# The expert stage on one Trainium2 core: per-expert lists of 64 slots, two experts side by side in the array, weights multiplied as plain 32-bit numbers

## The chip, the cores and the metric

The kernel runs on 1 core of one Trainium2 chip. The metric is device time in microseconds (us) from the first to the last instruction of one execution. TensorE (PE) does the matrix products, VectorE (DVE), ScalarE (ACT) and GpSimd (POOL) the elementwise work; SyncE (SP) only issues transfers. PEld is the loading of PE's stationary operand, which runs beside PE.

## The reference, cut to what matters

One block with a mixture of experts is followed by two layers of another block (dense feed-forward networks "ffn" and mixers). The change is inside the experts: 256 tokens of 1024 features, 16 experts in 4 groups, each expert with three 32-bit weight matrices (gate and up 1024 x 512, down 512 x 1024, 6 MB in all, 96 MB for the 16).

```
pg = softmax(t @ w_group + b_group); gsel = argmax(pg)           # one group per token
pe = softmax((t @ w_expert + b_expert)[the 4 experts of gsel])
top_p, top_i = top_k(pe, 2)                                       # two experts of that group
gates = one_hot(...) * pg_sel * top_p / sum(top_p)
for e in range(16):
    h = silu(t @ w_gate[e]) * (t @ w_up[e])
    y = y + gates[:, e:e + 1] * (h @ w_down[e])
```

A token uses 2 of 16 experts, so an expert has 32 tokens on average. In the drawn inputs the largest group has 80 tokens and the largest expert 43.

## The kernel before

The token rows lie in two tiles X[0], X[1] of 128 tokens by 1024 features. Phases run in a fixed order: `block1` (the first mixer, ending with `out_proj`), `moe` (the experts, `_moe`), then `ffn` and `mix` of the two later layers. Instructions are written in program order with two kinds of raised priority (`AHEAD` for loads, `urgent` for short work that frees a bank), and a scheduler makes one fixed order for each engine out of it; at run time each engine goes through its order and waits on semaphores.

Weights come in chunks of 1 MB (128 partitions x 2048 numbers) through SP's queue. Eight places hold raw chunks during the experts: 5 called `more`, 3 called `raw`. In `load`, ACT copies a chunk, 1024 columns at a time, into a rounded "high" part (`hi`, type fp32r), DVE subtracts to get the "low" part (`lo`), and a raw place is free when its parts are made. There are 5 places for `hi` and 5 for `lo`. A product of 32-bit accuracy is then three PE products, high by high, high by low, low by high (`mm3`).

For the experts, `moe_enter` turns X into high and low parts token by token and computes the router's products while `out_proj` finishes; `route` finds the group of each token and its place in the group's list of 128 slots; `moe_pass` builds a selection matrix `pm`, gathers the features of the slots by products with it (`gather`), and goes through the experts one by one: `half` (gate, then up), `hidden` (silu and gate weight), `hidden_T` (transposes) and `down`. All 128 slots of a group pass through each of its four experts, and the slot's gate weight is 0 where the token did not choose the expert. The outputs of the four experts add up in two banks `acc`; once per group `place` scatters them back into X. Then the first weights of the next ffn are fetched (`load_apart`, `prefetch`), and a second pass stands behind a branch that is taken only if a group has over 128 tokens (not the case here).

Of the kernel before, what the change touches and what calls it, by code (L numbers as in the profile page):

```python
# [10 lines left out]
F32 = mybir.dt.float32  # L11
# [8 lines left out]
P = 128  # L20
# [11 lines left out]
NMORE = 5  # L32


# ---------------------------------------------------------------- host layout
# [170 lines left out]
class Kern:  # L206
# [50 lines left out]
    # weights: one transfer, then exact high and low parts  # L257
# [21 lines left out]
    def load_apart(self, ap):  # L279
        """the same with its parts among the places of more_raw"""  # L280
# [18 lines left out]
    def rsqrt(self, out, ss, scale, n, pool=True):  # L299
        """out = (ss * scale + EPS) ** -0.5 for small [128, n]"""  # L300
# [10 lines left out]
    def newton(self, out, v, y, c):  # L311
        """out = v ** -0.5; y, c: places"""
# [31 lines left out]
    def half_parts(self, h):  # L344
        """places for high and low parts of four tiles of 128 features"""
# [6 lines left out]
    def enter(self, h):  # L352
        """for the phase to come: half h of X^T with its gain per feature, split"""
# [21 lines left out]
    def inv_rms(self, pool=True):  # L375
        """1 / rms of the rows of X: [128, TB]"""
# [11 lines left out]
    def bcast(self, inv, pool=None):  # L388
        """per-token scalars [128, TB] as rows over all partitions [128, T]"""
# [13 lines left out]
    def final_norm(self, fp):  # L403
        """X * its 1 / rms * gain; returns the product of 1 / rms before and after"""
# [11 lines left out]
    def _ffn(self, fp, ap, final):  # L416
# [4 lines left out]
        # the first gate and up tiles start on the first half of X^T  # L421
# [63 lines left out]
    # ------------------------------------------------------------ block 1  # L485
# [6 lines left out]
    def projA(self, w_ap, xh, xl, tag="wk", between=None):  # L492
        """512 output columns, token-major: two banks"""
# [12 lines left out]
    def _block1(self, mp):  # L506
# [3 lines left out]
        # values, token-major  # L510
# [24 lines left out]
        # lower bound of the forget gate  # L535
# [13 lines left out]
        # hgrn2: f, q feature-major  # L549
# [31 lines left out]
        # fox projections and the gate, between the levels of hgrn2  # L581
# [48 lines left out]
        # hgrn2 output  # L630
# [84 lines left out]
    def fox_cum(self, mp, xh, xl, invb):  # L715
        """cumulative log forget per head, as rows"""
# [26 lines left out]
    def values65(self, mp):  # L743
        """values of 8 heads with a column of ones each, 96 columns readable from every head on"""
# [92 lines left out]

    def moe_enter(self, n, t):
        """half n of X[t] is final: its parts, token-major, and a step later its transposes and router products"""
# [33 lines left out]
        with self.urgent():  # L873
            nc.scalar.copy(hi[:, t], x)
            (nc.gpsimd if last else nc.vector).tensor_tensor(lo[:, t], x, hi[:, t].bitcast(F32), op=OP.subtract)

    def _moe(self, mp):
        nc = self.nc
        with self.urgent():
            inv = self.inv_rms(False)  # L880
# [7 lines left out]
        with self.tc.If(n > P):  # L888
            self.moe_pass(mp, R, 1)
        self.ready, self.nmore = ready, NMORE  # L890

    def first_max(self, mp, name, p, also=None):
        """largest of 4 and the one-hot of its first place: p [128, TB, 4]"""
        nc = self.nc
        m = mp.tile([P, TB, 1], F32, name=name + "m")
        nc.vector.tensor_reduce(m[:, :, 0], p, axis=AX.X, op=OP.max)
        sc = mp.tile([P, TB, 4], F32, name=name + "s")
        nc.vector.tensor_tensor(sc, p, m.to_broadcast([P, TB, 4]), op=OP.is_equal)
        nc.vector.tensor_tensor(sc, sc, self.cfs("w4").unsqueeze(1).to_broadcast([P, TB, 4]), op=OP.mult)
        ms = mp.tile([P, TB, 1], F32, name=name + "k")  # L900
        nc.vector.tensor_reduce(ms[:, :, 0], sc, axis=AX.X, op=OP.max)
        oh = mp.tile([P, TB, 4], F32, name=name + "o")
        if also is not None:
            nc.vector.tensor_tensor(also, sc, ms.to_broadcast([P, TB, 4]), op=OP.is_equal)
        nc.vector.tensor_tensor(oh, sc, ms.to_broadcast([P, TB, 4]), op=OP.is_equal)
        return m, oh

    def route(self, mp, inv):
        nc = self.nc
# [4 lines left out]
        L = mp.tile([P, TB, 20], F32, name="L")  # L914
# [964 lines left out]
```

## Time and profile before

| | |
|---|---|
| median of 3 runs | 1732.8 us (1731.53 to 1735.16) |
| the profiled execution, its span | 1732.4 us |
| PE busy | 97% of the span |
| ACT, DVE, POOL busy | 54%, 73%, 10% |
| bytes moved by transfers | 320.43 MB, 185 GB/s on average |
| experts: first gather product to last addition to X | 182.6 to 485.5 us |

The span is the whole of the profiled execution; it lies 0.4 us under the median of the runs. Busy shares are averages over all phases, and PE's rows overlap each other, since the next product starts before the one before it has left the array; the distance between starts is therefore the better measure of a product's cost.

### The profile page before, as it was taken

The page shows a single profiled execution, that of the slowest core. Times are in us where ns is not written, and L with a number is a line of the kernel's source. Part 1 is how long each engine was busy: PE and PEld are TensorE (multiplying, and loading weights), DVE is VectorE, ACT ScalarE, POOL GpSimd, SP SyncE. Part 2 cuts the span into 40 slices and gives each one's busy share as a digit, 9 for nine tenths or more (in the row PEclk, how much of TensorE's full clock was granted, in tenths as well). Part 3 has the DMA queues.
Part 4 walks back from the last instruction along what each step waited for, and adds up shares of the span by engine and source line. Part 5 has one row for each costly group of instructions (what it writes and reads, how often), then busy time and mean ns, then how long its engine had stood idle before and what let it go on. Part 6 is the DMA issues. An engine that isn't in the chain of part 4 may idle for free.

```text
span 1732.4 us, 26642 instructions
## 1 busy us (share of the span) xinstructions
PE 1673.2 (97%) x10679; PEld 1484.0 (86%) x10679; DVE 1261.2 (73%) x1829; ACT 939.9 (54%) x1409; POOL 176.7 (10%) x149
## 2 busy tenths in 40 slices
PE   8998799999989999999899999999999999899999
PEld 7986688887789998999679999899998997689998
DVE  5966889998866567888776565665658987876655
ACT  5545577776754445755445444544448554454443
POOL 0321100000000000122440000000001215320000
PEclk9999899999999999999899999999999999999999
DMA  9332599998685532543225555555554432245552
GB/s 383 112 101 87 201 348 360 364 351 310 244 315 177 176 137 90 181 138 113 91 73 178 188 188 177 171 180 183 194 171 151 168 122 98 73 148 184 191 183 99
DMA packets 46212, 320.43 MB, mean 185 GB/s; under 512 B 5376, under 2 KB 5632, under 8 KB 8704
## 3 DMA queue, kind: packets, MB, share of 16 engines
q1 hardware_dynamic: 45504, 318.04, 51.6%
q8 instruction: 86, 1.41, 0.3%
q10 hardware_dynamic: 576, 0.60, 0.1%
q14 instruction: 46, 0.38, 0.1%
HBM read 317.58 MB, written 1.05 MB: 184 GB/s over the span
## 4 chain that ended last, share of the span: by engine, by line
PE 61%; DVE 7%; ACT 2%; issue 1%; POOL 0%; ACTq 0%; DVEq 0%
PE wk L295 10%; PE wk L296 10%; PE wk L297 10%; PE acc L295 9%; PE acc L297 9%; PE acc L296 9%; DVE lo L274 1%; ACT hi L273 1%; PE wk L1759 1%; DVE xs L1336 1%; PE wk L1740 1%; DVE ol L1402 1%; PE wk L1524 0%; DVE m L1533 0%; PE wk L340 0%
## 5 line engine op out<-in xcount | busy, mean ns | idle before, releaser
L274 DVE TENSOR_TENSOR lo<-raw,hi 128x1024 fp32r<-128x1024 f32 (+1 forms) x380 | 458.7, 1223 | 208.2 <-ACT hi L273 202.5
L273 ACT CAST hi<-raw 128x1024 fp32r<-128x1024 f32 (+2 forms) x414 | 426.2, 1044 | 337.9 <-PE wk L296 121.7
L295 PE MATMUL wk<-xh,hi 128*128 128x256 f32 x1344 | 380.9, 283 | 0.0
L297 PE MATMUL wk<-xh,lo 128*128 128x256 f32 x1344 | 380.3, 283 | 0.0
L296 PE MATMUL wk<-xl,hi 128*128 128x256 f32 x1344 | 380.3, 283 | 0.0
L296 PEld LDWEIGHTS wk<-xl,hi 128*128 128x128 f32 x1344 | 256.7, 191 | 1.8
L295 PEld LDWEIGHTS wk<-xh,hi 128*128 128x128 f32 x1344 | 256.7, 191 | 1.7
L297 PEld LDWEIGHTS wk<-xh,lo 128*128 128x128 f32 x1344 | 256.7, 191 | 0.0
L274 DVE TENSOR_TENSOR lo<-more,hi 128x1024 fp32r<-128x1024 f32 x184 | 222.3, 1239 | 46.9 <-ACT hi L273 44.7
L273 ACT CAST hi<-more 128x1024 fp32r<-128x1024 f32 x186 | 190.1, 1049 | 81.3 <-PE acc L297 26.1
L295 PE MATMUL acc<-xh,hi 128*128 128x256 f32 x688 | 199.6, 292 | 0.1
L297 PE MATMUL acc<-xh,lo 128*128 128x256 f32 x688 | 194.8, 283 | 1.7 <-DVE lo L274 1.7
L296 PE MATMUL acc<-xl,hi 128*128 128x256 f32 x688 | 194.8, 284 | 0.5 <-DVE xl L370 0.4
L295 PE MATMUL acc<-hi,hh 128*128 128x512 f32 x352 | 139.5, 398 | 0.4 <-ACT hh L445 0.3
L296 PE MATMUL acc<-lo,hh 128*128 128x512 f32 x352 | 138.6, 395 | 0.0
L297 PE MATMUL acc<-hi,hl 128*128 128x512 f32 x352 | 137.4, 395 | 0.0
L295 PEld LDWEIGHTS acc<-xh,hi 128*128 128x128 f32 x688 | 131.1, 191 | 3.1 <-issue 1.3
L297 PEld LDWEIGHTS acc<-xh,lo 128*128 128x128 f32 x688 | 131.5, 191 | 2.4 <-DVE lo L274 2.2
L296 PEld LDWEIGHTS acc<-xl,hi 128*128 128x128 f32 x688 | 131.6, 191 | 1.9 <-DVE xl L370 0.9
L296 PE MATMUL wk<-lo,xgh 128*128 128x512 f32 x248 | 98.2, 396 | 2.0 <-DVE lo L274 1.8
L295 PE MATMUL wk<-hi,xgh 128*128 128x512 f32 x248 | 99.0, 399 | 0.0
L297 PE MATMUL wk<-hi,xgl 128*128 128x512 f32 x248 | 98.1, 396 | 0.0
(462 smaller groups left out, 2747.3 us busy)
## 6 DMA issues: line engine op xcount, KB each, us to landing
raw<-in_ffn_dram SPq DMA_DIRECT2D x111, 1024.0 KB, 4.8
more<-in_wmoe_dram SPq DMA_DIRECT2D x60, 1024.0 KB, 6.0
raw<-in_win_dram SPq DMA_DIRECT2D x37, 1024.0 KB, 4.8
raw<-in_wmoe_dram SPq DMA_DIRECT2D x36, 1024.0 KB, 6.2
more<-in_ffn_dram SPq DMA_DIRECT2D x21, 1024.0 KB, 4.9
raw<-in_wout_dram SPq DMA_DIRECT2D x17, 1024.0 KB, 4.8
more<-in_win_dram SPq DMA_DIRECT2D x7, 1024.0 KB, 11.0
raw<-in_wlat_dram SPq DMA_DIRECT2D x4, 896.0 KB, 4.6
```

What stands on the lines that cost most here:

```text
L273: nc.scalar.copy(hi[:, :sub], raw[:, s])
L274: (eng or nc.vector).tensor_tensor(lo[:, :sub], raw[:, s], hi[:, :sub].bitcast(F32), op=OP.subtract)
L295: nc.tensor.matmul(out, ah, bh, start=start, stop=False)
L296: nc.tensor.matmul(out, ah, bl, start=False, stop=False)
L297: nc.tensor.matmul(out, al, bh, start=False, stop=stop)
L1336: nc.vector.scalar_tensor_tensor(o, xp[:, j, q:q + T], cwh[:, 12 * q + i:12 * q + i + 1], o, op0=OP.mult, op1=OP.add)
L1402: nc.vector.tensor_sub(hl, yn, hh.bitcast(F32))
L1740: nc.tensor.matmul(ps[:, j * T:(j + 1) * T], qT[:, h + j, t * P:(t + 1) * P], kT[:, h + j], start=True, stop=True)
L1759: nc.tensor.matmul(ps[:, j * 96:(j + 1) * 96], pt[:, i * P:(i + 1) * P], v[:, s, (h + j) * 65:(h + j) * 65 + 96], start=s == 0, stop=s == 1)
```

## The change

Tokens are listed per expert, not per group: `route` finds both chosen experts of every token and a place in each one's list of 64 slots (a further pass stands behind a branch for every further 64 tokens). Two experts of a group make a pair, 8 pairs in all. `two` multiplies for a pair: 64 slots of the first expert write partitions 0 to 63 of a bank through columns 0 to 63 of PE's array, 64 of the second write partitions 64 to 127 through columns 64 to 127. Both operands are plain 32-bit numbers (F32), so one product stands where three stood, and no chunk is split: `whole` loads a chunk into one of the 8 raw places, or as two halves into a place of `hi` and one of `lo`, 13 chunks in turn. ACT and DVE make no weight parts in this stage. Each pair's outputs are put into high and low parts and scattered once per two pairs. The gather is done per group, two feature tiles in one bank, with a plain 32-bit result. `inv_rms` before the router now uses POOL's power operation, and the last `xtl` subtraction moves from POOL to DVE. The extra passes lie behind the branch in another layout.

```diff
+NWHOLE = 13
+SLOTS = 64
...
+    def whole(self, ap, last=False):
+        self.wturn = (self.wturn + 1) % NWHOLE
+        with self.tc.high_priority(offset=AHEAD):
+            if last or self.wturn < NRAW + NMORE:
+                t = self.raw()
+                self.nc.sync.dma_start(t, ap)
+                return lambda a, n: t[:, a:a + n]
+            parts = []
+            for i, tag in enumerate(("hi", "lo")):
+                h = self.wp.tile([P, 1024], F32, name=f"whole{i}", tag=tag, bufs=5)
+                self.nc.sync.dma_start(h, ap[:, i * 1024:(i + 1) * 1024])
+                parts.append(h)
+            return lambda a, n: parts[a // 1024][:, a % 1024:a % 1024 + n]
...
-            (nc.gpsimd if last else nc.vector).tensor_tensor(lo[:, t], x, hi[:, t].bitcast(F32), op=OP.subtract)
+            if not last:
+                nc.vector.tensor_tensor(lo[:, t], x, hi[:, t].bitcast(F32), op=OP.subtract)
+        if last:
+            nc.vector.tensor_tensor(lo[:, t], x, hi[:, t].bitcast(F32), op=OP.subtract)
...
-            inv = self.inv_rms(False)
+            inv = self.inv_rms()
...
+    def more_passes(self, mp, R, n, p):
+        if p * SLOTS >= T:
+            return
+        with self.tc.If(n > p * SLOTS, preferred_fallthrough_block=False):
+            self.moe_pass(mp, R, p)
+            self.more_passes(mp, R, n, p + 1)
...
+        def two(out, x, c, wt, a, first, last):
+            for j in range(2):
+                h = slice(64 * j, 64 * j + 64)
+                nc.tensor.matmul(out[h], x[:, c + 64 * j:c + 64 * j + 64], wt[j](a, 512), start=first, stop=last)
...
             for c in range(2):
-                wt = self.load(w[6 * i + 2 * part + c], eng=None if i or part else nc.gpsimd)
+                wt = [self.whole(w[6 * (2 * i + j) + 2 * part + c], p or i == 7) for j in range(2)]
                 for k in range(4):
-                    self.mm3(ps, xgh[:, kk, sl], xgl[:, kk, sl], *wt(k * 512, 512), kk == 0, kk == KT - 1)
+                    two(ps, x[:, 4 * c + k], i % 2 * P, wt, k * 512, c == 0 and k == 0, c == 1 and k == 3)
...
-                    self.mm3(acc[n], hh[:, ks], hl[:, ks], *wt[c](k * 1024 + n * 512, 512),
-                             e == 0 and c == 0 and k == 0, e == 3 and c == 1 and k == 1)
+                    two(acc[n], ht, (2 * c + k) * P, wt[c], k * 1024 + n * 512, c == 0 and k == 0, c == 1 and k == 1)
+                if c == 1:
+                    yh, yl = (mp.tile([P, 512], F32R, name=f"y{a}{i % 2}{n}") for a in "hl")
+                    with self.urgent():
+                        nc.scalar.copy(yh, acc[n])
+                        nc.vector.tensor_sub(yl, acc[n], yh.bitcast(F32))
...
-        for i in range(17):
+        for i in range(9):
```

The order of the instructions shows it at two places. On PE, in a gate in the middle of the stage, before (`hi`, `lo` are parts of the weights, `xgh`, `xgl` of the gathered features):

```order
L295 MATMUL wk_2069<-hi_2072,xgh_1694 128x512
L296 MATMUL wk_2069<-lo_2073,xgh_1694 128x512
L297 MATMUL wk_2069<-hi_2072,xgl_1695 128x512
L295 MATMUL wk_2069<-hi_2072,xgh_1694 128x512
L296 MATMUL wk_2069<-lo_2073,xgh_1694 128x512
L297 MATMUL wk_2069<-hi_2072,xgl_1695 128x512
```

The same place now, the gate of the third pair (`more` and `whole0`, `whole1` hold the raw weights of the one and the other expert, `xg` the gathered features):

```order
L1077 MATMUL wk_2000<-more_2001,xg_1887 64x512
L1077 MATMUL wk_2000<-whole0_2003,xg_1887 64x512
L1077 MATMUL wk_2000<-more_2001,xg_1887 64x512
L1077 MATMUL wk_2000<-whole0_2003,xg_1887 64x512
L1077 MATMUL wk_2000<-more_2001,xg_1887 64x512
L1077 MATMUL wk_2000<-whole1_2005,xg_1887 64x512
```

Three products of 128 rows for one feature tile of one expert became two of 64 rows for one feature tile of two experts, and the products of the two experts alternate.

On SP's queue, where the loads of the expert weights begin, before:

```order
L268 DMA more_1538<-in_wout_dram 128x2048
L268 DMA raw_1763<-in_wmoe_dram 128x2048
L268 DMA raw_1849<-in_wmoe_dram 128x2048
L268 DMA raw_1871<-in_wmoe_dram 128x2048
L268 DMA more_1713<-in_wmoe_dram 128x2048
L268 DMA more_1909<-in_wmoe_dram 128x2048
```

And now:

```order
L270 DMA more_1538<-in_wout_dram 128x2048
L846 DMA raw_1725<-in_wmoe_dram 128x2048
L846 DMA raw_1757<-in_wmoe_dram 128x2048
L846 DMA raw_1759<-in_wmoe_dram 128x2048
L851 DMA whole1_1849<-in_wmoe_dram 128x1024
L851 DMA whole0_1847<-in_wmoe_dram 128x1024
L851 DMA whole1_1853<-in_wmoe_dram 128x1024
L851 DMA whole0_1851<-in_wmoe_dram 128x1024
L851 DMA whole0_1863<-in_wmoe_dram 128x1024
L851 DMA whole1_1865<-in_wmoe_dram 128x1024
L846 DMA more_1723<-in_wmoe_dram 128x2048
```

Three chunks in six halves, which wait for places that `out_proj` still uses, now stand ahead of `more_1723`, the first chunk that the stage multiplies with.

## Rows read from the trace of the kernel before

**Rows 1.** The page: engines, then GB/s of the transfers in 40 equal slices.

```profile
PE 1673.2 (97%) x10679; PEld 1484.0 (86%) x10679; DVE 1261.2 (73%) x1829; ACT 939.9 (54%) x1409; POOL 176.7 (10%) x149
...
GB/s 383 112 101 87 201 348 360 364 351 310 244 315 177 176 137 90 181 138 113 91 73 178 188 188 177 171 180 183 194 171 151 168 122 98 73 148 184 191 183 99
```

**Rows 2.** Busy time of each engine in five stretches, granted clock, transfer share, GB/s.

```profile
15.00:40.00 25.00, 24.95 (x172) 22.22 (x171) 15.92 (x32) 13.28 (x19) 0.00 (x0) 1.00 1.01 422
182.00:486.00 304.00, 296.60 (x1296) 237.34 (x1296) 267.42 (x281) 220.30 (x242) 0.00 (x0) 0.99 0.84 311
203.00:444.00 241.00, 237.19 (x1051) 191.75 (x1050) 216.51 (x208) 181.26 (x195) 0.00 (x0) 0.99 0.93 345
500.00:510.00 10.00, 10.00 (x86) 10.00 (x85) 6.93 (x9) 7.57 (x17) 0.69 (x1) 1.00 1.01 419
540.00:560.00 20.00, 20.00 (x147) 18.91 (x146) 12.28 (x16) 9.23 (x14) 0.00 (x0) 1.00 0.60 206
```

**Rows 3.** Groups of instructions by line from 182 to 486 us.

```profile
L274 DVE TENSOR_TENSOR lo<-more,hi 128x1024 fp32r<-128x1024 f32 x118 | 139.0, 1219 | 11.0 <-ACT hi L273 8.9 <-issue 1.6
L273 ACT CAST hi<-more 128x1024 fp32r<-128x1024 f32 x118 | 120.1, 1051 | 31.2 <-PE wk L297 16.1 <-PE acc L297 10.8 <-issue 1.5
L295 PE MATMUL wk<-hi,xgh 128*128 128x512 f32 x248 | 99.0, 399 | 0.0
```

**Rows 4.** PE in order of time, four stretches: start, length, engine, line, count.

```profile
149.44 0.39 PE L297 MATMUL acc<-hi,xl 128*128 128x512 f32 x1
149.67 0.39 PE L295 MATMUL acc<-hi,xh 128*128 128x512 f32 x1
...
162.04 1.92 PE L860 MATMUL wk<-more,wr 128*20 128x128 f32 x16
...
820.60 1.02 PE L1490 MATMUL wk<-xs 128*128 128x256 f32 x4
...
849.61 0.66 PE L1555 MATMUL wk<-m,xt 128*64 128x128 f32 x8
850.21 0.39 PE L1520 MATMUL wk<-mask_low,identb 128*128 128x512 bf16 x1
```

**Rows 5.** All engines in order of time between out_proj and the first gather.

```profile
168.76 4.74 POOL L274 TENSOR_TENSOR lo<-more,hi 128x1024 fp32r<-128x1024 f32 x2 [0.28 <-ACT hi L273]
168.96 2.25 DVE L303 TENSOR_SCALAR rsv<-ss 128x2 f32<-128x2 f32 x1
...
178.75 0.29 PE L916 MATMUL wk<-cf,Lt 20*128 20x20 f32 x1 [8.79 <-DVE Lt L912]
...
180.87 0.16 DVE L901 TENSOR_REDUCE pgk<-pgs 128x2 f32<-128x8 f32 x1
181.07 0.17 DVE L904 TENSOR_TENSOR ohb<-pgs,pgk 128x8 bf16<-128x8 f32 x1
...
182.63 0.77 PE L1003 MATMUL wk<-pm,xth 128*128 128x512 f32 x1 [1.07 <-DVE pm L992]
```

**Rows 6.** SP's queue in order of time; from the page one group of transfers.

```profile
203.24 12.95 SPq L268 DMA_DIRECT2D more<-in_wmoe_dram  x5
...
444.08 12.02 SPq L268 DMA_DIRECT2D more<-in_wmoe_dram  x4
...
raw<-in_win_dram SPq DMA_DIRECT2D x37, 1024.0 KB, 4.8
```

**Rows 7.** PE around its one stall inside the stage, and two stretches there.

```profile
424.54 0.52 PE L296 MATMUL wk<-lo,xgh 128*128 128x512 f32 x1 [1.77 <-DVE lo L274]
...
424.00:426.00 2.00, 1.46 (x4) 1.23 (x5) 2.00 (x3) 0.00 (x0) 0.00 (x0) 0.72 0.03 12
426.00:428.00 2.00, 2.00 (x6) 1.51 (x6) 2.00 (x3) 1.04 (x1) 0.00 (x0) 0.50 0.72 180
```

**Rows 8.** The end of the stage in order of time.

```profile
483.00 2.48 DVE L329 TENSOR_TENSOR X<-wk,X 128x512 f32<-128x512 f32 x4 [0.23 <-PE wk L1039]
...
489.47 0.88 PE L340 MATMUL wk<-cf,X 128*128 128x128 f32 x3 [5.82 <-PEq L888]
```

More of the change, by code (lines that the diff above doesn't have):

```diff
@@ new lines, in route @@
+        m1, o1 = self.first_max(mp, "p1", L.rearrange("p t g e -> p (t g) e"), TB * 5)
+        m1, o1 = (a.rearrange("p (t g) e -> p t g e", t=TB) for a in (m1, o1))
+        e2 = mp.tile([P, TB, 4, 4], F32, name="rp2")
+        for t in range(TB):
+            nc.vector.scalar_tensor_tensor(e2[:, t], o1[:, t, 1:5], NEG, L[:, t, 1:5], op0=OP.mult, op1=OP.add)
+        m2, o2 = self.first_max(mp, "p2", e2.rearrange("p t g e -> p (t g) e"), TB * 4)
+        m2, o2 = (a.rearrange("p (t g) e -> p t g e", t=TB) for a in (m2, o2))
@@ L1010, in moe_pass, with start @@
-        gather(0)
-        gather(1)
-        gs = mp.tile([P, 4, 5], F32, name="gslot")
-        def slot_gates():
+            pos = mp.tile([P, TB, 16, 1], F32, name="rpos2")
+            nc.vector.tensor_scalar(pos, R["pos"], float(-SLOTS * p), None, op0=OP.add)
+        gs = mp.tile([P, 8, 2], F32, name="gslot")
+        groups = {}
+        def start(g):
+            G = groups[g] = dict(pm=mp.tile([P, TB, 4 * SLOTS], F32R, name="pm", bufs=2),
+                                 x=mp.tile([P, KT, 4 * SLOTS], F32, name="xg", bufs=2),
+                                 pt=mp.tile([P, 2, T], F32R, name="pT", bufs=2), y=[])
+            with self.urgent():
+                for t in range(TB):
+                    nc.vector.tensor_tensor(G["pm"][:, t].rearrange("p (e s) -> p e s", e=4),
+                                            self.cfs("iota")[:, :SLOTS].unsqueeze(1).to_broadcast([P, 4, SLOTS]),
+                                            pos[:, t, 4 * g:4 * g + 4].to_broadcast([P, 4, SLOTS]), op=OP.is_equal)
@@ new lines, in gather @@
+        def gather(g, k):
+            pm, x = groups[g]["pm"], groups[g]["x"]
+            ps = self.bank()
+            for j in range(2):
+                hi, lo = self.xtok[(k + j) // 4]
+                s = slice((k + j) % 4 * P, ((k + j) % 4 + 1) * P)
+                r = ps[:, j * T:(j + 1) * T]
+                for t in range(TB):
+                    nc.tensor.matmul(r, hi[:, t, s], pm[:, t], start=t == 0, stop=False)
+                    nc.tensor.matmul(r, lo[:, t, s], pm[:, t], start=False, stop=t == 1)
+            with self.urgent():
+                nc.scalar.activation(x[:, k], ps[:, :T], AF.Copy, scale=self.col("ffn_norm", k))
+                nc.vector.tensor_scalar(x[:, k + 1], ps[:, T:], self.col("ffn_norm", k + 1), None, op0=OP.mult)
@@ L1024, in moe_pass @@
-        pt = mp.tile([P, 4, T], F32R, name="pT")
-        def place(g, n, y):
-            yh = mp.tile([P, 512], F32R, name="yh", bufs=2)
-            yl = mp.tile([P, 512], F32R, name="yl", bufs=2)
-            with self.urgent():
-                nc.scalar.copy(yh, y)
-                nc.vector.tensor_sub(yl, y, yh.bitcast(F32))
-            def scatter():
-                for t in range(TB):
-                    ps = self.bank()
-                    sl = pt[:, g, t * P:(t + 1) * P]
-                    nc.tensor.matmul(ps, sl, yh, start=True, stop=False)
-                    nc.tensor.matmul(ps, sl, yl, start=False, stop=True)
-                    self.add_to_X(t, n, ps, 1.0)
-            return scatter
@@ L1043, in half @@
-        def half(i, part):
-            sl = slice(i // 4 * P, (i // 4 + 1) * P)
-            ps = self.bank("wk" if i or part else "acc")
+                    nc.tensor.matmul(ps[:, 6 * i:6 * i + 6], G["pm"][:, t, i * P:(i + 1) * P],
+                                     R["gp"][:, t, 2 * g + i].rearrange("p a b -> p (a b)"), start=t == 0, stop=t == 1)
+            gv = mp.tile([P, 2, 2, 3], F32, name="gsv", bufs=2)
+            nc.vector.tensor_copy(gv.rearrange("p i a b -> p (i a b)"), ps[:, :12])
@@ L1047, in half @@
+            nc.scalar.copy(G["pt"].rearrange("p i t -> p (i t)"), ps)
+        def two(out, x, c, wt, a, first, last):
+            for j in range(2):
+                h = slice(64 * j, 64 * j + 64)
+                nc.tensor.matmul(out[h], x[:, c + 64 * j:c + 64 * j + 64], wt[j](a, 512), start=first, stop=last)
+        def half(i, part, between=None):
+            x = groups[i // 2]["x"]
+            ps = self.bank()
             for c in range(2):
-                wt = self.load(w[6 * i + 2 * part + c], eng=None if i or part else nc.gpsimd)
+                wt = [self.whole(w[6 * (2 * i + j) + 2 * part + c], p or i == 7) for j in range(2)]
@@ L1049, in half @@
                 for k in range(4):
-                    kk = 4 * c + k
-                    self.mm3(ps, xgh[:, kk, sl], xgl[:, kk, sl], *wt(k * 512, 512), kk == 0, kk == KT - 1)
-                    if i == 0 and part == 0 and kk < KT - 2:
-                        gather(kk + 2)
+                    if between is not None and k % 2 == 0:
+                        between(4 * c + k)
+                    two(ps, x[:, 4 * c + k], i % 2 * P, wt, k * 512, c == 0 and k == 0, c == 1 and k == 3)
             return ps
@@ new lines, in place @@
+        def place(g, n):
+            G = groups[g]
+            y = [a for a in G["y"] if a[0] == n]
+            for t in range(TB):
+                ps = self.bank()
+                for q, (_, i, yh, yl) in enumerate(y):
+                    sl = G["pt"][:, i, t * P:(t + 1) * P]
+                    nc.tensor.matmul(ps, sl, yh, start=q == 0, stop=False)
+                    nc.tensor.matmul(ps, sl, yl, start=False, stop=q == 1)
+                self.add_to_X(t, n, ps, 1.0)
+        start(0)
@@ L1102, in moe_pass @@
+        for k in (0, 2):
+            gather(0, k)
+        h = None
+        for i in range(9):
+            if i < 8:
+                gate = half(i, 0, (lambda k: gather(0, k + 4) if k < 4 else None) if i == 0 else None)
             if i == 0 and p == 0:
```

208 lines of the change are left out of this document (85 added, 123 removed).

## The prediction

> **What bounds the kernel now.** I read the page first, then the expert stage by stretches, then its groups of instructions, then single places in order of time. The page says that PE is busy for 97% of the span and that the transfers peak in the slices after the fifth [rows 1]: those are the experts. There PE is busy 296.6 of 304 us, and in the stage's steady part the transfers' engines are busy 93% of the time as well [rows 2]. So two things stand close together, PE just ahead. PE's share of it: 16 experts make 72 products each (three for every product of the algorithm), 1152 in all, and a product of 512 columns starts 0.23 us after the one before it [rows 4], which is 265 us of the 303 from the first gather to the last addition to X [rows 5, 8]; gathers, scatters and transposes fill most of the rest. ACT and DVE are off the path: making parts takes them about 2 x 96 x 1.05 = 202 us and 2 x 96 x 1.22 = 234 us [rows 3], and PE waits for it almost nowhere. The transfers: 80 chunk issues lie between 203.24 and 444.08 us [rows 6], 3.01 us per chunk, because a place comes free only as fast as PE eats. When the queue is always full, 15 to 40 us and 500 to 510 us, the same 16 engines move 419 to 422 GB/s [rows 2], which is 2.49 us for a chunk of 1.05 MB.
>
> **What a product costs after the change.** The trace has plain 32-bit products at other places, and each shows as two records. The router's 16 records (L860, 128 columns) take 1.92 us: with 0.27 for the last one's own length, 0.110 us from start to start. The four of L1490 (256 columns) take 1.02 us, 0.21 from start to start [rows 4]. So a record costs 0.84 ns per column, 0.428 us for 512 columns, and a plain product 0.856 us, 1.24 times the three that it replaces (0.69). Alone this would be a loss; what decides is whether the two experts of a pair run at once. L1555 shows that: it writes 64 rows of a bank for one head and the other 64 for another, as `two` does. Its eight records of 128 columns take 0.66 us. One after the other they would take 7 x 0.110 + 0.27 = 1.04, two at a time 3 x 0.110 + 0.27 = 0.60. It is the second [rows 4]. I take full overlap, 0.856 us for a pair of products; the other bound is 1.71.
>
> **PE's sum.** Eight pairs make 16 + 16 + 16 products each, 384, that is 192 couples x 0.856 = 165 us. The gathers are 128 products of 256 columns; 540 to 560 us has 147 products of 256 and 512 columns in 20 us, so at most 0.136 each [rows 2], 17 us. The scatters: 64 x 0.23 = 15 us. 48 transposes at 0.110 and 16 small products: 6 us. Going over to 64 columns and back: L1555's block holds PE from 849.61 to 850.21, 0.60 us, of which four steps of 0.110 explain 0.44 [rows 4]; 0.16 for each way there and back, and the new order has 58 changes, so 29 x 0.16 = 5 us. Sum 208 us instead of about 300.
>
> **The head.** Before, PE waits 8.79 us for `Lt`, because DVE's small operations of `inv_rms` take 2.25 us each while POOL subtracts weight parts (4.74 us for two) [rows 5]; elsewhere such an operation takes 0.16. The change takes the subtraction off POOL, and the chain of small operations off DVE. `route` gets longer: some 28 small operations instead of 10 between `L` and `pm`, 0.20 us apart [rows 5], 3.6 us more. First gather at about 178.5 instead of 182.63: 4 us won. Were POOL's power operation slow, or the longer `route` to cost 0.3 us each, it is 0.
>
> **The transfers' sum.** Thirteen chunks fit ahead; they are loaded while `out_proj` ends and `route` runs. The six halves ahead of `more_1723` wait for `hi` and `lo` of `out_proj`, whose last product is over before the rows at 168.76 [rows 5]; even if all four chunks came only then, 4 x 2.49 + 2.3 brings them to about 181, so this costs 0 to 3 us; I take 0. Then 83 chunks remain. The first place comes free after the first gathers and four couples, about 8.5 us with the clock still low after the wait in `route`, at 187. A lone chunk lands 4.8 us after its issue [rows 6]: 192. The 82 others follow at the rate of a full queue. No row shows loads in rows of 4 KB, as the halves are, so I take 2.55 us instead of 2.49: 82 x 2.55 = 209, the last lands at 401. PE alone would be done at 178.5 + 4 + 208 = 390, so it waits for the transfers, by little. Behind the last chunk stand four couples (3.4), parts and scatter of the last half, the additions to X: 7 us, 408. For uneven arrival and short falls of the clock I add 4: 412. Behind it nothing changes: the first ffn chunks are queued right behind the last expert chunk, and the 5.82 us that PE waits at the branch [rows 8] I leave, by 2 either way.
>
> So the stage ends at 412 instead of 485.5, 73.5 us earlier; 1732.4 - 73.5 = 1658.9 for the profiled execution, and the median of the runs lay 0.4 above it: 1659 us. The work that ACT and DVE lose (202 and 234 us) gains nothing by itself, since PE and the transfers covered it. If PE had to wait for nothing, the end would be near 397 (1644); that is the lower bound.
>
> **Rivals.** *The transfers get no faster.* Then a chunk costs 2.83 us (345 GB/s at a share of 0.93 makes 371 at a full one) or the 3.01 of now [rows 2, 6]: 82 x 0.28 = 23 or 82 x 0.46 = 38 us later, 1682 to 1697. For it speaks that inside this stage no long stretch was faster; against it that the queue was never full there. The Trainium skill speaks for this rival: "DMA: Bandwidth & Descriptors", section Specifications, gives a core about 358 GB/s of the HBM; by that a chunk takes 2.93 us and the time would be 1690. The trace does not agree, with 422 and 419 GB/s over 25 and 10 us [rows 2].
>
> *PE's clock.* Now PE hardly pauses. With a pair's two chunks eaten in 3.4 us and arriving in 5.1, it will pause about every 5 us in gate and up. One pause of 1.77 us is followed by 0.72 and 0.50 of the clock, that is by the lower of its two levels, 1.2 GHz [rows 7]. If half the stage ran so, PE's 208 us would be 208 / 0.75 = 277, the end 463, the time 1710. Against it: at the low level PE is slower than the transfers, has no pause, and in the trace the clock is back at 1.00 within the stage. The skill names this case in "TensorE: Matmul & The Clock Gate", section HAM oscillation: a kernel that waits for weights between short bursts falls back to the lower clock at every tile.
>
> *Slower: the couples do not overlap with 512 columns* as they do with 128, for instance since two streams of 32-bit numbers from SBUF are too much over so long a time. Then 384 x 0.856 = 329, with the other 43 us of PE the end is at 178.5 + 4 + 372 + 3 = 557, 72 us later: 1804. It decides against the change from 1.34 us per couple on (192 x 1.34 + 43 = 300).
>
> *It does not do what it says:* a second pass, if an expert had over 64 tokens; the largest has 43.
>
> **How the numbers follow.** Forecast 0.66, transfers no faster 0.17, clock 0.10, no overlap 0.06, no change for another reason 0.01. The likeliest gives 1659. The lower bound 1645 is PE without waits, the upper 1697 takes in the slow transfers; the rest of the clock and the non-overlap stay out. About 0.2% is what a measurement of this kernel can tell from no change. Faster 0.92 (forecast, transfers, most of the clock), same 0.02, slower 0.06.
>
> **What would show it.** Right: records of L1077 of 64 rows start in twos, some 0.43 us from two to two; transfers at 400 GB/s or more from about 190 to 400 us; SP waiting for PE, not DVE; no `hi` or `lo` casts there; the first gather near 178; X's last addition near 412. Wrong: records 0.43 us apart one by one; a share under 0.95 while PE also waits; long stretches at clock 0.5.

## The result and the profile after

The changed kernel takes 1661.2 us (median of 4 runs, 1655.7 to 1664.6) against 1732.2 before, a ratio of 0.9585 (95% interval 0.9564 to 0.9606): 71 us faster, where 74 were forecast (1659.0, range 1645 to 1697). The profiled execution has a span of 1658.1 us. Where its 74.2 us against the profiled 1732.4 lie is worked out from the starts of the same instructions in both traces:

| stretch | before, us | after, us | won | forecast |
|---|---|---|---|---|
| start to the last product of `out_proj` | 165.2 | 163.1 | 2.1 | 0 |
| from there to the first gather | 17.5 | 10.4 | 7.1 | 4 |
| first gather to the last addition to X | 302.8 | 231.1 | 71.7 | 69.5 |
| last addition to X to the 24th product of the ffn | 10.3 | 14.6 | -4.3 | 0, by 2 either way |
| the rest | 1236.6 | 1239.0 | -2.4 | 0 |

The first and the last stretch hold the same work in both kernels; over all profiles of this study the last product of `out_proj` lies between 163.1 and 165.5 us and the rest lasts 1233 to 1239, so the 2.1 and 2.4 us there lie within what one execution differs from another. The three in the middle are the change.

The page of the kernel after, its engines and its GB/s in 40 slices (before: [rows 1]):

```profile
PE 1605.6 (97%) x10407; PEld 1344.7 (81%) x10407; DVE 1031.5 (62%) x1645; ACT 747.2 (45%) x1219; POOL 166.3 (10%) x145
...
GB/s 381 136 77 133 330 415 417 417 417 352 288 187 187 72 136 165 153 106 99 76 153 204 178 182 187 165 180 191 174 167 153 153 120 84 77 156 200 178 193 87
```

DVE lost 230 us of work and ACT 193, PE only 68, and PE's share of the span is 97% as before. PE's share tells nothing of what ends the stage now; the GB/s do. Four slices in a row now stand at 415 to 417. The same in stretches of the stage (busy time of each engine, granted clock, transfer share, GB/s; before: [rows 2]):

```profile
178.00:190.00 12.00, 12.00 (x61) 5.31 (x61) 2.52 (x9) 2.57 (x4) 0.00 (x0) 0.96 0.46 181
190.00:400.00 210.00, 206.96 (x937) 84.62 (x934) 32.53 (x61) 26.34 (x47) 0.00 (x0) 0.98 1.01 413
...
357.00:362.00 5.00, 4.76 (x12) 1.49 (x14) 0.41 (x1) 0.58 (x1) 0.00 (x0) 0.50 1.02 423
...
410.00:415.00 5.00, 1.34 (x6) 1.34 (x7) 1.36 (x3) 1.36 (x3) 0.00 (x0) 0.50 1.00 390
```

From 190 to 400 us the 16 transfer engines have no gap. PE looks just as full there, but its rows overlap; what a product costs is read from the starts. PE in order of time, from four places of the stage:

```profile
179.37 0.59 PE L1077 MATMUL wk<-more,xg 128*64 128x512 f32 x1
179.38 0.59 PE L1077 MATMUL wk<-raw,xg 128*64 128x512 f32 x1
179.80 0.59 PE L1077 MATMUL wk<-more,xg 128*64 128x512 f32 x1
...
188.25 7.09 PE L1077 MATMUL wk<-more,xg 128*64 128x512 f32 x32
195.17 7.04 PE L1077 MATMUL wk<-whole,xg 128*64 128x512 f32 x32
...
252.83 1.07 PE L1077 MATMUL wk<-whole,xg 128*64 128x512 f32 x2
253.83 0.50 PE L1131 MATMUL wk<-yh,pT 128*128 128x512 f32 x1
...
357.24 1.12 PE L1077 MATMUL acc<-more,mht 128*64 128x512 f32 x1 [3.04 <-DMA more<-in_wmoe_dram]
357.25 1.12 PE L1077 MATMUL acc<-raw,mht 128*64 128x512 f32 x1
358.15 1.06 PE L1077 MATMUL acc<-more,mht 128*64 128x512 f32 x1
```

The records of the two experts start in twos, 0.01 us apart, 0.43 us from two to two, as forecast. (A couple is the pair of products, one of each expert, that `two` issues.) At 252.83 a single product, two records, stands between scatters: here the order tears a couple apart, and its two products run alone. At 357.24 PE has waited 3.04 us for a chunk, the couples behind it start 0.86 us apart, and the stretch 357 to 362 us shows clock 0.50, the lower of its two levels (1.2 GHz).

The head, all engines in order of time (before: [rows 5]):

```profile
166.85 0.17 DVE L305 TENSOR_SCALAR rsv<-ss 128x2 f32<-128x2 f32 x1
167.10 0.69 POOL L307 TENSOR_TENSOR inv<-rsv,nhalf 128x2 f32<-128x2 f32 x1 [46.22 <-DVE rsv L305]
...
168.58 0.38 DVE L946 SCALAR_TENSOR_TENSOR L<-wk,inv,rowt 128x20 f32<-128x20 f32 x2 [0.33 <-PE wk L944]
...
172.66 0.19 DVE L970 SCALAR_TENSOR_TENSOR rpos<-wk,rsel 128x32 f32<-128x32 f32 x1
...
173.45 0.55 PE L1046 MATMUL wk<-pm,xth 128*128 128x256 f32 x1 [0.83 <-DVE pm L1033]
```

From `rsv` to the end of `inv` it takes 0.95 us; the chain of small operations before took 10.8, of which the four that ran beside POOL took 2.25 or more each. The end of the stage (before: [rows 8]):

```profile
397.20 0.26 PEld L1077 LDWEIGHTS acc<-more,mht 128*64 128x64 f32 x3 [0.17 <-DMA more<-in_wmoe_dram]
...
402.11 2.47 DVE L331 TENSOR_TENSOR X<-wk,X 128x512 f32<-128x512 f32 x4
404.50 2.35 DVE L291 TENSOR_TENSOR more<-raw,more 128x1024 fp32r<-128x1024 f32 x2
...
407.12 1.64 PE L342 MATMUL wk<-cf,X 128*128 128x128 f32 x9 [4.14 <-DVEq L916]
...
413.12 0.88 DVE L372 SCALAR_TENSOR_TENSOR xl<-wk,fin,xh 128x256 fp32r<-128x256 f32 x2 [6.28 <-issue]
...
413.66 0.58 PE L298 MATMUL acc<-xl,more 128*128 128x256 f32 x1 [4.49 <-DVE xl L372]
```

The last chunk is there at 397.20, X is complete at 404.58. Then something is new: DVE still subtracts for the first ffn chunk (L291), passes the branch after it, and does nothing for 6.28 us ("issue": the profile shows nothing that it waits for). PE, through the branch at 407.12, waits 4.49 us for DVE, and 410 to 415 us show clock 0.50.

### The profile page after: what moved, and what is told of

Same layout as the page of the kernel before. It is cut to its first block, busy times and chain, and to the rows that moved or that the text cites. A ratio compares the mean times of both kernels' runs of the same rounds, so it can differ in the third digit from the quotient of the medians.

```text
span 1658.1 us, 25503 instructions
## 1 busy us (share of the span) xinstructions
PE 1605.6 (97%) x10407; PEld 1344.7 (81%) x10407; DVE 1031.5 (62%) x1645; ACT 747.2 (45%) x1219; POOL 166.3 (10%) x145
## 4 chain that ended last, share of the span: by engine, by line
PE 62%; DVE 9%; ACT 2%; issue 2%; POOL 0%; ACTq 0%; DVEq 0%
PE wk L297 10%; PE wk L298 10%; PE wk L299 10%; PE acc L297 9%; PE acc L299 9%; PE acc L298 9%; DVE lo L276 2%; DVE xs L1370 1%; ACT hi L275 1%; PE wk L1793 1%; PE wk L1774 1%; DVE ol L1436 1%; PE wk L1558 0%; DVE m L1567 0%; DVE q L1741 0%
## 5 line engine op out<-in xcount | busy, mean ns | idle before, releaser
L276 DVE TENSOR_TENSOR lo<-raw,hi 128x1024 fp32r<-128x1024 f32 (+2 forms) x312 | 378.4, 1224 | 203.1 <-ACT hi L275 199.0
L275 ACT CAST hi<-raw 128x1024 fp32r<-128x1024 f32 (+1 forms) x344 | 354.7, 1042 | 329.3 <-PE wk L298 125.6
L276 DVE TENSOR_TENSOR lo<-more,hi 128x1024 fp32r<-128x1024 f32 x64 | 81.1, 1276 | 33.2 <-ACT hi L275 32.8
L275 ACT CAST hi<-more 128x1024 fp32r<-128x1024 f32 x64 | 66.0, 1044 | 48.1 <-PE wk L298 18.4
L436 DVE TENSOR_TENSOR gu<-wk,invb 128x512 f32<-128x512 f32 x84 | 58.0, 691 | 47.3 <-PE wk L299 47.2
L276 POOL TENSOR_TENSOR lo<-raw,hi 128x1024 fp32r<-128x1024 f32 x32 | 76.6, 2398 | 94.2 <-ACT hi L275 94.2
L447 ACT CAST hh<-h 128x256 fp32r<-128x256 f32 x88 | 35.7, 406 | 101.9 <-DVE h L444 101.8
## 6 DMA issues: line engine op xcount, KB each, us to landing
whole<-in_wmoe_dram SPq DMA_DIRECT2D x66, 512.0 KB, 12.6
more<-in_win_dram SPq DMA_DIRECT2D x7, 1024.0 KB, 13.6
```

Of the source, the lines that this page charges most:

```text
L275: nc.scalar.copy(hi[:, :sub], raw[:, s])
L276: (eng or nc.vector).tensor_tensor(lo[:, :sub], raw[:, s], hi[:, :sub].bitcast(F32), op=OP.subtract)
L436: nc.vector.tensor_tensor(gu, gate.rearrange("p (a t) -> p a t", a=2), invb.unsqueeze(1).to_broadcast([P, 2, T]), op=OP.mult)
L447: nc.scalar.copy(hh, h)
```

## The experiments

My theory: the couples overlap, so that PE alone would need some 210 us, and the transfers, always at a full queue, end the stage at 397 plus a tail; the head was won by taking the weights' subtraction off POOL; 4 us are given back at the branch because DVE comes late. The rivals: PE ends the stage, the overlap is not what pays, 13 places are what keeps the queue full, the power operation is what won the head. Because executions differ by 2 us up to the last product of `out_proj`, stretches are given from that point:

| kernel | time, us | to the first gather | to the last addition to X | from there to the 24th ffn product |
|---|---|---|---|---|
| before | 1732.2 | 17.5 | 320.3 | 10.3 |
| after | 1661.2 | 10.4 | 241.5 | 14.6 |
| all_columns | 1791.8 | 10.4 | 379.4 | 12.3 |
| half_loads | 1634.0 | 10.4 | 220.9 | 11.0 |
| half_products | 1651.3 | 10.4 | 238.1 | 11.7 |
| one_after_other | 1670.7 | 10.4 | 251.7 | 14.0 |
| whole8 | 1667.4 | 10.4 | 251.6 | 13.7 |
| inv_newton | 1662.8 | 11.2 | 244.9 | 15.4 |
| pool_subtract | 1658.7 | 10.4 | 242.4 | 15.1 |
| pool_busy | 1664.3 | 18.2 | 248.5 | 13.6 |
| ffn_parts_pool | 1653.2 | 10.4 | 242.4 | 9.6 |
| halves_once | 1656.0 | 10.4 | 247.0 | 9.4 |
| first_place | 1655.1 | 10.4 | 248.1 | 9.2 |
| branch_default | 1654.5 | 10.4 | 243.9 | 11.5 |

The first four experiments and pool_busy have one time each; the others are medians of 4 or 5. The stage itself, whose work is the same in after, pool_subtract, ffn_parts_pool and branch_default, ends between 241.5 and 243.9 us there, so differences of 2 to 3 us in the last column but one say little.

**all_columns.** Do the columns side by side pay?

```diff
-                h = slice(64 * j, 64 * j + 64)
-                nc.tensor.matmul(out[h], x[:, c + 64 * j:c + 64 * j + 64], wt[j](a, 512), start=first, stop=last)
+                nc.tensor.matmul(out, x[:, c:c + P], wt[j](a, 512), start=first and j == 0, stop=last and j == 1)
```

> Part changed: every product of the two experts uses all 128 columns of the array and both write the same 128 rows, so the two experts' results are added into one another; loads, order and number of products stay. Theory (the products of a pair run at once, and this saves half of 384 x 0.86 us): one product of 512 columns starts 0.86 us after the other (two records 0.43 apart), 384 of them take 329 us instead of 165, the stage ends near 404.6 + 165 - 20 (what the pairs lose now at their block edges and in one stall) = 550 us, the time is 1795 to 1810. Rival (the columns are not what makes it fast; two 64-row products run one after the other at half the cost): the stage ends where it does now, 1655 to 1665.

1791.8 us, 3 below the theory's interval and far from the rival. The groups of instructions, first this kernel, then the changed one (busy us, mean ns of one):

```profile
L1076 PE MATMUL wk<-more,xg 128*128 128x512 f32 x216 | 99.2, 592 | 0.0
```

```profile
L1077 PE MATMUL wk<-more,xg 128*64 128x512 f32 x216 | 69.5, 597 | 0.0
```

One record lasts the same, 592 or 597 ns; only the starts differ. All 768 records take 325 us from start to start here and 185 in the changed kernel. Nor do narrow records follow each other any faster when they run alone: in one_after_other, below, they start 0.43 us apart. So the narrow product is no cheaper by itself: the gain over this kernel is that two run at once. Without it the change is nearly 60 us slower than the kernel before.

**half_loads and half_products.** Which of the two ends the stage?

```diff
-                wt = [self.whole(w[6 * (2 * i + j) + 2 * part + c], p or i == 7) for j in range(2)]
+                wt = [self.whole(w[6 * (2 * i + j) + 2 * part + c], p or i == 7) for j in range(1)] * 2
```

and the same for the chunks of `down` in half_loads; in half_products

```diff
-                    two(ps, x[:, 4 * c + k], i % 2 * P, wt, k * 512, c == 0 and k == 0, c == 1 and k == 3)
+                    if k % 2 == c:
+                        two(ps, x[:, 4 * c + k], i % 2 * P, wt, k * 512, c == 0 and k == 0, c == 1 and k == 3)
...
-                for k in range(2):
+                for k in (c,):
```

> Part changed: the second expert of a pair uses the chunks of the first, so only 48 of the 96 chunks are loaded; the number and form of products stay. Theory (transfers end the stage, and PE is close behind: its starts in the stage of the changed kernel add up to 229 us, of which about 8 go with one wait for a chunk and some 8 with couples that the order tears apart): the wait and the low clock behind it go, the last addition to X comes at 390 to 398 us, the time is 1642 to 1652, with the transfers' share near 0.5. Rival 1 (PE alone sets the end): 403 to 405, 1656 to 1660. Rival 2 (reading weights while transfers write them slows PE): couples start less than 0.42 us apart, end before 385.

> Part left out: half of the products of gate, up and down (192 of 384); all 96 chunks are loaded. Theory (transfers end the stage at 2.53 us per chunk): the first place comes free a few us earlier, 83 chunks follow at 415 GB/s, the last lands at 388 to 397, the last addition to X at 393 to 402, the time is 1645 to 1657. Rival (PE ends the stage and the transfers only follow it): the end moves by about half of the products' 165 us, to some 325 us, 1580.

half_loads, stretch and first group; half_products, stretch and PE's longest waits (us in total, times, longest):

```profile
190.00:380.00 190.00, 190.00 (x931) 77.78 (x928) 36.37 (x64) 29.60 (x51) 0.00 (x0) 1.00 0.57 196
```

```profile
L1077 PE MATMUL wk<-more,xg 128*64 128x512 f32 x192 | 45.0, 600 | 0.0
```

```profile
190.00:390.00 200.00, 157.34 (x532) 57.50 (x529) 31.15 (x59) 25.06 (x44) 0.00 (x0) 0.92 1.02 417
```

```profile
PE acc L1077 <- DMA more<-in_wmoe_dram: 11.9, 6, 5.6
PE wk L1077 <- DMA more<-in_wmoe_dram: 11.4, 6, 3.9
PE acc L1077 <- DMA whole<-in_wmoe_dram: 6.8, 3, 4.6
```

With half of PE's products gone the stage ends 3.4 us earlier, hardly more than the spread of 2.4, and PE waits for transfers again and again: the transfers end it, at 417 GB/s. With half of the loads gone it ends 20.6 us earlier, more than I expected (7 to 15), and 1634.0 us lies below the interval; the end at 384.85 is even the one that rival 2 named, but its other sign, couples closer than 0.42 us, is not there. PE waits for no transfer, and from the first gather to the end of the last scatter it needs 384.0 - 174.4 = 209.6 us. So PE's work needs 20 us less than it takes in the changed kernel, which its busy share, 99 and 100% in the two kernels, does not show. Where the 20 are in the changed kernel: its blocks of couples add up to 184.7 us, here to 167.8; 7.8 of the 17 stand in the one block with the wait of 3.04 us and the low clock, most of the others where the order tears couples apart, which it does not do in half_loads. The other 3 to 4 us of the 20.6 lie outside the blocks. Couples start no closer than 0.43 us here either, so PE is as fast beside 413 GB/s as beside 196.

**one_after_other.** Must the two products stand next to each other?

```diff
+                for j in range(2):
+                    for k in range(4):
+                        two(ps, x[:, 4 * c + k], i % 2 * P, wt, k * 512, c == 0 and k == 0, c == 1 and k == 3, (j,))
...
-            for j in range(2):
+            for j in js:
```

> Changed: the order of products alone. Four (in the down products two) of the first expert are issued in a row, then as many of the second, instead of alternating. Theory A (only a product that stands directly behind the other one in PE's order runs beside it): each run of eight records overlaps with the next at its border alone, the couples cost nearly 0.86 us per product, 1770 to 1805. Theory B (PE takes a waiting product of the other columns from further back, as the pairs of L1555 before, which stood in the order 0, 0, 64, 64): starts in twos as now, 1655 to 1665.

Neither interval held 1670.7, but it lies near theory B. PE in order of time where a block begins (`whole` is the first expert, `more` the second):

```profile
209.94 2.36 PE L1077 MATMUL wk<-whole,xg 128*64 128x512 f32 x5
211.72 0.64 PE L1077 MATMUL wk<-more,xg 128*64 128x512 f32 x1
212.14 0.59 PE L1077 MATMUL wk<-whole,xg 128*64 128x512 f32 x1
212.19 0.59 PE L1077 MATMUL wk<-more,xg 128*64 128x512 f32 x1
```

In PE's order eight records of `whole` stand ahead of the first of `more`. The first four run alone; the first of `more` starts beside the fifth, ahead of three that stand before it. So PE takes a product of the other columns from some four records further back, and each block pays about 2 us for its lead. Its 17 blocks add up to 197 us; the stage ends 10 us later, and it is PE that ends it here: from 172 us to the end of the stage it waits for no transfer.

**whole8.** Are 13 places needed to keep the queue full?

```diff
-NWHOLE = 13
+NWHOLE = 8
```

> Changed: 8 chunks in turn instead of 13 (no chunk goes as two halves into places of hi and lo). Theory (a full queue needs only a few chunks ahead; the five more places pay because they are filled before the first product): five chunks less lie ready at the start, so 5 x 2.53 = 12.6 us later with the rate still at 410 GB/s or more, last addition to X at 415 to 420, 1670 to 1677. Rival (the depth keeps the queue full): the rate falls to the 345 to 371 GB/s of the kernel before, 88 x 0.28 to 0.46 us more on top, 1695 to 1715.

1667.4 us (ratio 0.9624, 0.9605 to 0.9643), a little below the theory's interval; the stage ends 10.1 us later, not 12.6. The stretch:

```profile
190.00:390.00 200.00, 189.54 (x856) 76.54 (x854) 30.18 (x57) 24.39 (x43) 0.00 (x0) 1.00 1.01 421
```

421 GB/s with 8 places against 413 with 13: loads in rows of 8 KB move 2% more than those with halves of 4 KB among them, at the same full share. This run changes the depth and the rows at once, but the changed kernel has both kinds of load in one full queue: from 200 to 392 us a chunk in one piece lands 2.49 us after the one before it, a chunk in two halves 2.56 (medians). So the rows, not the depth, explain the rate; the five more places pay because they are full when PE begins, 5 x 2.5 = 12.5 us, less what the halves cost.

**The head: inv_newton, pool_subtract, pool_busy.**

The first, the second, and what the third adds to the first:

```diff
-            inv = self.inv_rms()
+            inv = self.inv_rms(False)
```

```diff
-            nc.vector.tensor_tensor(lo[:, t], x, hi[:, t].bitcast(F32), op=OP.subtract)
+            nc.gpsimd.tensor_tensor(lo[:, t], x, hi[:, t].bitcast(F32), op=OP.subtract)
```

```diff
+        z = mp.tile([P, 1024], F32, name="busy")
...
+            for t in (1, 1, 1, 1):
+                nc.gpsimd.tensor_tensor(z, self.X[t], self.X[0], op=OP.subtract)
```

> Undone: inv_rms before the router is again a chain of small operations on DVE instead of one power operation of POOL; the subtraction stays on DVE. Theory (the chain was slow only because POOL subtracted at the same time): some ten operations at 0.1 to 0.2 us instead of 0.17 + 0.69, first gather at 174 to 175.5 instead of 173.4, time 1660 to 1665. Rival (the chain itself is what the change took away): first gather at 178 or later, 1666 to 1670.

> Undone: the last subtraction that makes xtl is again on POOL; inv_rms stays on POOL's power operation. Theory (POOL's subtraction of 4.7 us is the head's loss): DVE's operations that run beside it take up to 2 us each instead of 0.2, or the power operation queues behind it; first gather at 177 to 182, and since the first place comes free later by as much, the whole stage too: 1665 to 1670. Rival (transfers hide the head, since 13 places are filled by then): first gather later, end of the stage within 1 us of 404.6, 1659 to 1663.

> Added to inv_newton: four subtractions of 128 x 1024 on POOL, as long as the four of the kernel before, into a scratch tile that nobody reads; inv_rms is DVE's chain of small operations. Theory (what made the chain slow before was POOL's long subtractions beside it): each of DVE's small operations that falls beside one of them takes 2.2 to 2.3 us instead of 0.16, three to five of them, and the first gather comes 16 to 21 us after the last product of out_proj instead of 11.2. Rival (the chain was slow for another reason of the kernel before, such as its loads): 11 to 12 us.

The power operation is worth 0.8 us (11.2 instead of 10.4). Moving the last `xtl` subtraction is worth nothing: 10.4 in both, so my expectation for pool_subtract was wrong, and not for the rival's reason; the subtraction is short (1.26 us on POOL, not the 4.7 of my expectation, which are the weights' two), and nothing in the head waits for it. What was won is shown by pool_busy: with POOL busy again and the chain on DVE the head takes 18.2 us, 7.0 more than the 11.2 of inv_newton. (Before the change it was 17.5, with a shorter `route` and four of the chain's operations held, not two.) DVE and POOL in this kernel:

```profile
166.87 10.16 POOL L903 TENSOR_TENSOR busy<-X,X 128x1024 f32<-128x1024 f32 x4 [43.51 <-DVE X L331]
```

```profile
170.11 0.67 DVE L1810 COPY more<-wk 128x512 f32<-128x512 f32 x1
...
172.24 0.17 DVE L305 TENSOR_SCALAR rsv<-ss 128x2 f32<-128x2 f32 x1
172.44 2.19 DVE L316 TENSOR_SCALAR rsc<-rsv 128x2 int32<-128x2 int32 x1
174.66 0.17 DVE L317 TENSOR_SCALAR rsy<-rsc 128x2 int32<-128x2 int32 x1
174.87 2.18 DVE L319 TENSOR_TENSOR rsc<-rsy 128x2 f32<-128x2 f32 x1
```

An operation on two numbers per partition takes 2.19 us when it meets POOL's 2.5 us subtraction, 0.16 when not. The Trainium skill states a lock that fits ("Trainium Architecture — The Big Picture", section What this means for kernel authors): of the engines only DVE and GpSimd contend for SBUF, and by an exclusive lock, not by a shared rate. These rows agree: DVE's operation is not slowed in proportion but held until POOL's is through, for POOL's third and fourth subtraction end at 174.60 and 177.03 us and DVE's two at 174.63 and 177.05. Not every operation of DVE is held: the copy at 170.11, out of a bank that PE wrote, takes its usual 0.67 us beside POOL's second, and so do the four additions from banks at 405.25 in ffn_parts_pool, below, which take 2.47 us beside POOL and take 2.47 without it (402.11, above).

**ffn_parts_pool and branch_default.** Why does PE wait behind the branch?

```diff
-            nc.vector.tensor_sub(lo[:, s], raw[:, s], hi[:, s].bitcast(F32))
+            nc.gpsimd.tensor_tensor(lo[:, s], raw[:, s], hi[:, s].bitcast(F32), op=OP.subtract)
```

and on top of it in branch_default

```diff
-        with self.tc.If(n > p * SLOTS, preferred_fallthrough_block=False):
+        with self.tc.If(n > p * SLOTS):
```

> Changed: the low part of the first ffn chunk, made at the end of the stage, on POOL instead of DVE (two subtractions). Theory (DVE comes to the branch 2.3 us late behind these two, its code is then fetched behind three chunks of weights, PE waits 4.5 us for DVE's next work and goes on at half clock): that wait and the low clock go, 4 to 7 us won against the changed kernel, 1653 to 1658. Rival (the code fetch takes that long anyway, and POOL's 2.4 us per piece are late for the ffn's low products): at most 2 us won, 1659 to 1664.

> Undone against ffn_parts_pool: the layout of the branch (the extra passes stand behind it in the other way, as before). Theory (with the layout of before PE waits at the branch longer): from the last addition to X to PE's first product behind it 4 us, as before, instead of 2.5; 1653 to 1657. Rival (the layout does nothing): 2.5 us, 1651 to 1655.

1653.2 us (ratio 0.9538, 0.9524 to 0.9552): 8 us under the changed kernel's median, of which the profiles show 5.0 at this place; the other 3 are not located. All engines in order of time:

```profile
405.25 2.47 DVE L331 TENSOR_TENSOR X<-wk,X 128x512 f32<-128x512 f32 x4
405.63 4.67 POOL L291 TENSOR_TENSOR more<-raw,more 128x1024 fp32r<-128x1024 f32 x2 [235.56 <-SPq L916]
...
410.24 3.65 PE L342 MATMUL wk<-cf,X 128*128 128x128 f32 x16 [4.14 <-issue]
...
411.88 0.48 DVE L372 SCALAR_TENSOR_TENSOR xl<-wk,fin,xh 128x256 fp32r<-128x256 f32 x1 [4.15 <-ACT xh L371]
```

DVE is through the branch 4.2 us after its last addition to X, ready when ACT is, and PE does its 16 transposes without a stop. branch_default: PE comes back 5.4 us after the last addition to X instead of 2.5, and its 24th product 2.0 us later; 1654.5 us, whose interval (0.953 to 0.9562) contains the other. So the layout saves some 2 to 3 us at this branch by the profile, too little for the times to show. What DVE does in the 6.28 us is not settled. My guess is that its next instructions come late, behind the three ffn chunks issued at 405.43 to 406.49 us: between 407 and 413.2 us the profile has three packets in the queues that it marks "instruction", while the transfers move 385 GB/s in all. No run took only these chunks away.

**halves_once and first_place.** Two attempts at a faster version, on top of ffn_parts_pool:

```diff
-        self.wturn = (self.wturn + 1) % NWHOLE
+        self.wturn += 1
-            if last or self.wturn < NRAW + NMORE:
+            if last or self.wturn < NRAW + NMORE or self.wturn >= NWHOLE:
```

and on top of that in first_place

```diff
-                gate = half(i, 0, (lambda k: gather(0, k + 4) if k < 4 else None) if i == 0 else None)
+                gate = half(i, 0, (lambda k: (gather(0, 4), gather(0, 6)) if k == 4 else None) if i == 0 else None)
```

> Changed against ffn_parts_pool: chunks go as halves into places of hi and lo only for the first 13; from then on the 8 whole places alone are used in turn. Theory (the queue needs no more than 8 places to stay full, and loads in rows of 8 KB run at 421 GB/s instead of 414 with the halves): 83 chunks x 0.04 us = 3 us earlier, 1648 to 1652. Rival (13 places in turn are needed): PE waits several times, the rate falls below 414, 1655 to 1665.

> Changed against halves_once: the 16 gathers of features 4 to 7 of the first group come behind the four couples of the first chunk instead of between them. Theory (the transfers stand still until the first place is free, and every us there moves the end): the first place is free 2.5 to 3.5 us earlier, and so is the end, 1645 to 1650. Rival (the pause of transfers at the start is made up for by PE's wait, or PE ends the stage): no change, 1648 to 1652.

Both missed: 1656.0 (0.9545 to 0.9573) and 1655.1 us (0.9535 to 0.9573), no better than 1653.2. The first time lies in its rival's interval, but not for the rival's reason. halves_once in three stretches:

```profile
190.00:200.00 10.00, 10.00 (x48) 3.30 (x46) 0.75 (x1) 1.16 (x2) 0.00 (x0) 1.00 1.00 394
200.00:220.00 20.00, 20.00 (x106) 8.92 (x104) 2.68 (x5) 3.06 (x6) 0.00 (x0) 1.00 0.67 260
220.00:380.00 160.00, 150.61 (x679) 62.72 (x676) 25.79 (x50) 19.84 (x35) 0.00 (x0) 1.00 1.01 421
```

The steady rate is 421, as expected. But while PE eats the five chunks that lie in halves, no place in use comes free, and from 200 to 220 us the queue is dry a third of the time: 20 x 0.33 = 6.6 us lost, once, against 3 won. In first_place the first place is free only 1.1 us earlier, since the clock's low stretch at the start now falls on the couples (0.85 us from two to two) instead of on gathers, and the end does not come earlier (248.1 against 247.0).

## Why the prediction was right

**The couples' overlap** held at 512 columns as at 128: 0.43 us from two to two. The rival without overlap would have given 1804; the run that has no overlap took 1792.

**PE's sum** of 208 us was right to 2: 209.6 in half_loads, with the low clock of the first gathers, for which the prediction adds 4 us without a row (212 in all); the couples 167.8 with their edges where I had 165 and a share of the 5 us for going over. What I did not foresee is that the order would tear couples apart and PE would so lose most of its distance to the transfers.

**The transfers' sum** was right, and the time rests on it. The first refill was issued at 183.86 (187 forecast), 10.4 us behind the first gather where I had 8.5; the last chunk was there at 397.20 (401). With 4.8 us for the first to land, 82 chunks took 208.5 us, 2.54 each. The 2.55 of the forecast was an allowance without a row, but its reason held: the halves cost more (2.56 against 2.49, under whole8). The rival of slower transfers, by the Trainium skill's 358 GB/s ("DMA: Bandwidth & Descriptors", section Specifications), does not hold here: 413 to 421 GB/s over 200 us, with this one core at work.

**The tail** of 7 us was right (7.4); the 4 us for uneven arrival were not needed. Once the stage was under way the clock fell once, behind the wait of 3.04 us, to 0.50 for some 6 us; by the last chunk PE had caught up and waited for it (0.17 us at 397.20), so this cost nothing. The clock's rival was wrong in how often PE would pause. Its price of twice the time held for the couples at the low level (0.86 us instead of 0.43), but half a stage at that level was never seen: even half_products, where PE pauses again and again, shows 0.92 from 190 to 390 us.

**The head** is a term that I mis-sized: 7.1 us won instead of 4. I had taken `route`'s longer chain at 3.6 us more; it is 2.8 (5.65 us from `inv` to the first gather instead of 2.9). And the chain of small operations lost 9.8 us where my 4 + 3.6 allowed 7.6.

**The step that failed** is the last: "Behind it nothing changes ... the 5.82 us that PE waits at the branch I leave, by 2 either way". PE's wait at the branch fell to 4.14, but DVE's work behind it came late, and 4.3 us were given back. The cause was to be seen in the order of the changed kernel: DVE's two subtractions for the ffn chunk stand behind the additions to X. DVE in order of time there, in the kernel before:

```profile
478.91 2.35 DVE L289 TENSOR_TENSOR more<-raw,more 128x1024 fp32r<-128x1024 f32 x2
```

That was 4 us ahead of the additions to X. I looked at what moves inside the stage and not at what its end finds unfinished.

So the stage ended 7.4 us earlier than forecast, of which 2.1 stand ahead of the last product of `out_proj` and belong to the spread of executions; 6.7 were given back behind it, 4.3 at the branch and 2.4 in that spread. The sum fits better than its terms, and that it fits to 2 us is in part luck: a head 3 us too small and a branch 4.3 us too cheap nearly cancel.

## What to carry to other kernels

A product that is 1.24 times dearer can still pay if half of the array's columns do other work at the same time; price it by the distance of starts, never by the busy share, which said 97% before and after and hid 20 us. When PE is relieved, ask at once what the transfers can do with the queue always full: here that number, from two stretches of the trace before where it was full, gave the last chunk's landing within 4 us. And at the end of a stage that got shorter, look on every engine for work that the old length used to hide.

## What the runs showed of the hardware

- A matmul of the second half of the columns overtook three records of the first half that stood ahead of it in PE's order (one_after_other), but not more: its lead of four records ran alone.
- 8 chunks in turn feed the queue as well as 13 (421 and 413 GB/s). Rows of 4 KB instead of 8 cost 3% (2.56 us against 2.49 for a chunk, in the same queue); in the mix of both that is 2%.
- A small DVE operation beside a POOL subtraction of 128 x 1024 waits for all of it (2.18 to 2.29 us instead of 0.16); DVE copies and additions out of PE's banks do not (0.67 us, and 2.47 for four, with POOL and without).
- PE and transfers do not disturb each other here: couples of 0.43 us with transfers at 196 and at 413 GB/s.
